# A two-layer hybrid decoder on one core: the first norm's scale and bias moved behind the transposition, throwaway products ahead, another order of first loads and splits

## The chip, the core and the metric

The kernel runs on one core of a Trainium2 chip. Its engines are TensorE (PE, with its weight loads as PEld), VectorE (DVE), ScalarE (ACT), GpSimd (POOL) and SyncE (SP, which here only issues DMAs). Each engine takes its instructions in the order in which the program issues them, and waits for the others by semaphores. The metric is the device time of one execution in microseconds; lower is better.

## The reference

Two layers of attention and gated MLP on 256 positions of 1,024 channels, with a LayerNorm ahead of the first layer and one behind each half of a layer:

```python
h = _layer_norm(x, ln_in_g, ln_in_b)              # the first norm
for l in range(DEPTH):                            # DEPTH = 2, ALPHA = 4 ** 0.25
    mix = _hybrid_mixer(h, positions, weights_of(l))   # x @ w_in, three attention branches, gates, w_out
    h = _layer_norm(ALPHA * h + mix, ln1_g[l], ln1_b[l])
    ffn = _conv_gated_mlp(h, w_up[l], conv_w[l], conv_b[l], w_down[l])
    h = _layer_norm(ALPHA * h + ffn, ln2_g[l], ln2_b[l])

def _layer_norm(x, g, b):                         # mean and var over the channels
    return (x - mean) * rsqrt(var + 1e-5) * g + b
```

The first norm's result is used twice: transposed, as the operand of all input projections of layer 0, and untransposed, in `ALPHA * h + mix`. Branch A of the mixer is softmax attention with a causal mask and a forget term: scores of a block of 128 queries, softmax, and the product with the values.

## The kernel before, in words

The 256 positions are two blocks (tb 0 and 1) of 128 rows; a block is held as two tiles of 128x512 (`h00`, `h01`, `h10`, `h11`). Products are made at nearly full fp32 precision from fp32r operands: each operand is split into a high half (ACT copies it with rounding) and a low half (DVE or POOL subtracts the high half from the original), and a product is three matmuls: high by high, low by high, high by low.

Weights are streamed from one flat array in order of use (class `Stream`): SP loads `raw` tiles (7 buffers), and each 128x512 piece is split into an `hl` tile (16 buffers; hl0 is the first piece). A `raw` buffer comes free when its pieces are split, an `hl` buffer when its products are done. `unit_x` takes 8 pieces and makes for both blocks a result of 128 rows by 512 columns: 48 matmuls of 128x512. `unit_x_tbfirst`, used for the first unit of each layer, makes all 24 of block 0 before those of block 1, since block 1's norm comes later.

The order of instructions is laid down when the program is built. `Tasks` holds generators for the side work (norms, rotary, softmax, ...); each `T.tick()` between matmuls advances every one by one step and lets the stream split another piece. `ready(...)` holds a task back by a rough clock of each engine (`Clocks`) until its inputs should be there. `T.until(cond)` ticks, without issuing products, until a condition holds. So what a task issues stands in the engine's queue wherever the building of the program was at the time, and the engine meets it there.

The start: ACT loads the identity, the positions and the rotary frequencies; SP loads block 0 of x, then `ln_in_g` and `ln_in_b` broadcast to all 128 rows, then two `raw` tiles, block 1, and more `raw`. `ln_half` makes the statistics, `ln_stats` the factor `rs` (a power on POOL), `ln_apply` four two-operand instructions of 128x512 on DVE with the broadcast scale and bias, and `ln_tail` transposes the tiles on PE (4 of 128x128 each, into a PSUM bank `att`), and writes the transposed operand as high half `hTh` (ACT) and low half `hTl` (DVE). Then `rotary_tables` (16 small POOL instructions and two sines on ACT between two table loads), the small loads and the mask constants follow.

Branch A (`task_A`) of layer 0 is added to the tasks behind the unit for its keys, and runs beside the unit for its values (`av`) and the first gate unit. Its scores, the transposition of the softmax's result `p` and the product with the values stand in PE's queue between the products of units. Behind `av` the program takes new `lng` and `lnb` tiles for the norm behind the mixer.

Of the kernel before, what the change touches and what calls it, by code (L numbers as in the profile page):

```python
# [10 lines left out]
F32 = mybir.dt.float32  # L11
R32 = mybir.dt.float32r
BF16 = mybir.dt.bfloat16
# [5 lines left out]
P = 128  # L19
# [89 lines left out]
class Stream:  # L109


    def __init__(self, nc, ve, sc, clocks, flat, raw_pool, hl_pool, plan):
        self.nc, self.flat, self.raw_pool, self.hl_pool = nc, flat, raw_pool, hl_pool
        self.ve, self.sc, self.clocks = ve, sc, clocks
        self.hold, self.low = False, LOW
        self.dma_clk, self.free_at, self.split_at = 0.0, {}, {}
        self.chunks, self.items = [], []
        off = 0
        for (_, _, kts, cols) in plan:
            n = kts * cols  # L120
            c = len(self.chunks)
            self.chunks.append((off, n))
            off += P * n
            w = 512 if cols >= 512 else cols
            for q in range(n // w):
                self.items.append((c, q * w, w))
        self.raw, self.hl = {}, {}
        self.next_dma = self.next_split = self.used = self.freed = 0

# [158 lines left out]
def tile_hybrid(ctx: ExitStack, tc: tile.TileContext, a: dict, out: bass.AP):  # L288
# [23 lines left out]
    def nm(s):  # L312
        uid[0] += 1
        return f"{s}_{uid[0]}"
# [25 lines left out]
    def bc_load(t, src, n, off=0, q=gp):  # L340
        q.dma_start(t, bass.AP(tensor=src.tensor, offset=off, ap=[[0, P], [1, n]]))
# [24 lines left out]
    for q in range(2):  # L366
        nc.sync.dma_start(h[0][q], xv[:, 0, 512 * q:512 * q + 512])
    for q in range(2):
        bc_load(lng[:, 512 * q:512 * q + 512], a["ln_in_g"], 512, 512 * q, nc.sync)
        bc_load(lnb[:, 512 * q:512 * q + 512], a["ln_in_b"], 512, 512 * q, nc.sync)  # L370
    W.dma()
    W.dma()
    for q in range(2):
        nc.sync.dma_start(h[1][q], xv[:, 1, 512 * q:512 * q + 512])
    nc.sync.dma_start(cst[:, C_TRI:C_INVF], a["cst"][:, C_TRI:C_INVF])
    for _ in range(RAW_BUFS - 2):
# [7 lines left out]
    def small_loads():  # L384
        bc_load(bf, a["b_f"], DEPTH * 4, q=nc.sync)
        bc_load(kvg, a["kv_norm_g"], DEPTH * LATENT, q=nc.sync)
        bc_load(dg, a["diff_norm_g"], DEPTH * P, q=nc.sync)
        nc.sync.dma_start(convp, a["convp"])

    tri = cst[:, C_TRI:C_TRI + P]  # L390
    negid = cpool.tile([P, P], BF16, name="negid")
    m01 = cpool.tile([P, 256], BF16, name="m01")
# [23 lines left out]
    def rotary_tables():  # L416

        c1 = 6.28125
        c2 = float(np.float32(np.float32((2 * math.pi - c1) * 2 ** 20).astype(np.int64) / 2.0 ** 20))
        c3 = float(np.float32(2 * math.pi - c1 - c2))  # L420
        gp.tensor_copy(posf, posi)
        for t in range(2):
            gp.tensor_scalar(ang[:, t, :], cst[:, C_INVF:C_INVF + 16], posf[:, t:t + 1], None, ALU.mult)
        gp.tensor_scalar(rn, ang, 1.0 / (2 * math.pi), 12582912.0, ALU.mult, ALU.add)
        gp.tensor_scalar(rn, rn, 12582912.0, None, ALU.subtract)
        for c in (c1, c2, c3):
            gp.tensor_scalar(red, rn, -c, None, ALU.mult)
# [5 lines left out]
        yield  # L433
# [93 lines left out]
    def ln_tail(tb, st, hT, g, b, flag):  # L527
# [11 lines left out]
        flag.add(tb)  # L539
        W.hold = len(flag) < 2  # L540


    def unit_x(lhs, kts, ncols):

# [10 lines left out]
    def unit_x_tbfirst(lhs, kts, ncols, ready=None):  # L555
        bk = [acc(), acc()]
        ws = []
        for tb in range(2):
            if ready is not None:
                T.until(lambda: tb in ready)  # L560
            for k in range(kts):
                if tb == 0:
                    ws.append(W.take())
                lh, ll = lhs(k, tb)
                mm3(bk[tb][:, :ncols], lh, ll, ws[k][:, 0, :ncols], ws[k][:, 1, :ncols], k == 0, k == kts - 1)
                if tb == 1:
                    W.free()
                T.tick()
        return bk

    def unit_w(hT, bks):
# [29 lines left out]
    def layer(l, hT, hflag):  # L601
# [585 lines left out]
        return hT2, flag2  # L1187


    hT, hflag = new_hT(), set()  # L1190
# [6 lines left out]
    T.tick()  # L1197
    tables = rotary_tables()
    next(tables)
    T.until(lambda: 0 in hflag)  # L1200
    for i in range(4):
        W.refill(ve)
    for q in range(2):
        ln_half(1, q, sts[1])
    T.add(ln_tail(1, sts[1], hT, lng, lnb, hflag))
    W.low = LOW
    for i in range(4):
        W.refill((gp, gp, ve, gp)[i])
        T.tick()
    T.add(tables)  # L1210
    small_loads()
    masks()

    def task_lambdas():
        for _ in range(40):
# [12 lines left out]
def lay_out(inp):  # L1228
# [3 lines left out]
    for l in range(DEPTH):  # L1232
# [13 lines left out]
        for (n, k0, kts, cols) in plan:  # L1246
            m = mats[n][k0 * P:(k0 + kts) * P, :].reshape(kts, P, cols)
            parts.append(m.transpose(1, 0, 2).reshape(-1))
    return np.concatenate(parts)


# [25 lines left out]
```

## Time and profile before

| | |
|---|---|
| three timed runs | 935.33 us median (933.94 to 935.53) |
| the profiled execution, its own time | 935.33 us |
| its span in the profile | 933.5 us |
| PE busy in the span | 905.1 us, 97% |
| DVE, ACT, POOL busy | 656.0, 513.5, 47.3 us |
| mean granted clock of TensorE | 0.995 |

A page of the profile gives each engine's busy time, and answers to queries give the instructions in order of time, who waited for whom, and what ended each wait. All times below are microseconds from the start of the span. Where one row stands for several instructions (x4), its time is that from the first's start to the last's end. PE's matmuls are pipelined, so a row's time is longer than the distance to the next; what a product costs is read from that distance.

### The profile page before, as it was taken

Reading aid. Unit: us, or ns where it says so; the run is one execution under the profiler, and the core shown is the slowest. Engines: PE = TensorE matmul, PEld = TensorE weight load, DVE = VectorE, ACT = ScalarE, POOL = GpSimd, SP = SyncE. Lnnn points to the kernel's source line nnn. Section 1 sums busy time; section 2 is a strip of 40 time slices with the busy share of each in tenths; the row PEclk is TensorE's granted clock in tenths of the full one; section 3 lists DMA queues with packets and bytes.
Section 4 is the critical chain, followed back from the end, with each engine's and each line's share of the span. In section 5 each row is a group of like instructions: output and inputs, shape, how many; then the busy total and the mean of one; then the engine's idle time right before and its main releaser. Section 6 shows DMA issues by size and latency. Waiting matters only on the chain.

```text
span 933.5 us, 14405 instructions
## 1 busy us (share of the span) xinstructions
PE 905.1 (97%) x5306; PEld 791.1 (85%) x5306; DVE 656.0 (70%) x1270; ACT 513.5 (55%) x1008; POOL 47.3 (5%) x62
## 2 busy tenths in 40 slices
PE   4999999999999999999999999999999999999995
PEld 2877897888888999999988789888888799999994
DVE  7788677567678766666788966865667886766755
ACT  4654666655536655655456455765554375655541
POOL 6000010001000000000010000100110100000001
PEclk9999999999999999999999999999999999999998
DMA  8843256656535766566345332846665286566601
GB/s 306 275 141 113 69 178 232 188 193 194 181 121 207 245 194 189 172 197 190 113 159 180 123 113 70 298 143 201 192 197 171 87 298 196 181 194 188 182 3 45
DMA packets 46536, 161.45 MB, mean 173 GB/s; under 512 B 5697, under 2 KB 6209, under 8 KB 46465
## 3 DMA queue, kind: packets, MB, share of 16 engines
q1 hardware_dynamic: 44208, 154.94, 51.5%
q0 software_dynamic: 1408, 4.98, 1.7%
q8 instruction: 41, 0.67, 0.3%
q10 hardware_dynamic: 848, 0.60, 0.2%
q14 instruction: 31, 0.25, 0.1%
HBM read 159.46 MB, written 1.05 MB: 172 GB/s over the span
## 4 chain that ended last, share of the span: by engine, by line
PE 70%; issue 21%; DVE 6%; DMA 1%; POOL 1%; ACT 0%; SPq 0%; ACTq 0%; DVEq 0%; POOLq 0%
PE acc L240 49%; PE att L240 21%; DVE h L240 2%; DVE s L240 1%; DMA raw<-in_w_dram 1%; POOL rs L240 1%; DVE hl L240 1%; DMA cst<-in_cst_dram 1%; DVE bst L240 1%; DVE mx L240 0%; DVE mv L240 0%; DVE hTl L240 0%; DVE t L240 0%; ACT h L240 0%; POOL hl L240 0%
## 5 line engine op out<-in xcount | busy, mean ns | idle before, releaser
L240 DVE TENSOR_TENSOR hl<-raw,hl 128x512 fp32r<-128x512 f32 (+1 forms) x581 | 389.5, 696 | 191.3 <-ACT hl L240 189.7
L240 ACT ACTIVATE hl<-raw 128x512 fp32r<-128x512 f32 (+1 forms) x584 | 347.8, 625 | 189.5 <-PE att L240 92.4
L240 PE MATMUL acc<-hl,hTh 128*128 128x512 f32 (+1 forms) x896 | 285.9, 392 | 4.1 <-DVE hl L240 2.0
L240 PE MATMUL att<-hTh,hl 128*128 128x256 f32 x1280 | 231.3, 283 | 0.0
L240 PEld LDWEIGHTS att<-hTh,hl 128*128 128x128 f32 x1280 | 200.8, 192 | 1.4
L240 PEld LDWEIGHTS acc<-hl,hTh 128*128 128x128 f32 x896 | 168.3, 189 | 39.5 <-DVE hl L240 2.7
L240 PE MATMUL att<-hTl,hl 128*128 128x256 f32 x640 | 181.1, 283 | 0.0
L240 PE MATMUL acc<-hl,hTl 128*128 128x512 f32 (+1 forms) x448 | 173.3, 387 | 1.8 <-DVE hTl L240 1.8
L240 PE MATMUL acc<-hl,act 128*128 128x512 f32 x528 | 123.4, 390 | 0.0
L240 PEld LDWEIGHTS att<-hTl,hl 128*128 128x128 f32 x640 | 122.8, 192 | 0.0
L240 PEld LDWEIGHTS acc<-hl,act 128*128 128x128 f32 x528 | 97.9, 188 | 19.5
L240 PEld LDWEIGHTS acc<-hl,hTl 128*128 128x128 f32 x448 | 85.0, 190 | 17.8 <-DVE hTl L240 2.7
L240 PE MATMUL acc<-hl,oT 128*128 128x512 f32 x288 | 68.0, 391 | 0.0
L240 PEld LDWEIGHTS acc<-hl,oT 128*128 128x128 f32 x288 | 53.8, 188 | 11.0
L240 DVE SCALAR_TENSOR_TENSOR cv<-att,convp,cv 128x255 f32<-128x255 f32 x88 | 40.4, 480 | 15.4 <-ACT cv L240 13.9
L240 PE MATMUL acc<-hTh,hl 128*128 128x256 f32 x256 | 47.7, 287 | 0.0
L240 PE MATMUL acc<-hl,mT 128*128 128x512 f32 x192 | 45.4, 392 | 0.0
L240 ACT ACTIVATE hTh<-att 128x512 fp32r<-128x512 f32 x16 | 9.6, 598 | 59.2 <-PE att L240 59.1
L240 PEld LDWEIGHTS acc<-hl,mT 128*128 128x128 f32 x192 | 35.6, 188 | 7.1
L240 PEld LDWEIGHTS acc<-hTh,hl 128*128 128x128 f32 x256 | 39.8, 191 | 2.0 <-issue 1.7
L240 PE MATMUL acc<-hTl,hl 128*128 128x256 f32 x128 | 36.2, 283 | 0.0
L240 POOL TENSOR_TENSOR rs<-mv,mhalf 128x1 f32<-128x1 f32 x10 | 9.1, 906 | 482.4 <-DVE mv L240 482.4
(160 smaller groups left out, 696.6 us busy)
## 6 DMA issues: line engine op xcount, KB each, us to landing
raw<-in_w_dram SPq DMA_DIRECT2D x284, 512.0 KB, 4.2
raw<-in_w_dram SPq DMA_DIRECT2D x8, 332.0 KB, 4.4
lng<-in_ln_g_dram POOLq DMA_DIRECT2D x4, 512.0 KB, 4.0
lnb<-in_ln_b_dram POOLq DMA_DIRECT2D x4, 512.0 KB, 5.9
h<-in_x_dram SPq DMA_DIRECT2D x4, 256.0 KB, 4.9
lng<-in_ln_in_g_dram SPq DMA_DIRECT2D x2, 256.0 KB, 5.2
lnb<-in_ln_in_b_dram SPq DMA_DIRECT2D x2, 256.0 KB, 5.2
wu<-in_w_ukv_dram POOLq DMA_DIRECT2D x2, 256.0 KB, 3.0
```

Source lines behind the costliest of these rows:

```text
L240: f(*args, **kw)
```

## The change

Six things change.

1. The first norm. `first_norm` takes the place of `ln_tail` for the norm ahead of layer 0. DVE makes only `(x - mean) * rs` (one `tensor_scalar` per tile of 128x512); PE transposes that; and on the transposed bank, where channels are rows, the scale and bias are one number per partition each (`gb`, 128x16, a small DMA on ACT's queue). They are applied in place in PSUM, 128 columns at a time: 4 `tensor_scalar` on DVE per bank, for the last bank 4 activations on ACT. High and low halves are made behind that.
2. `h` itself gets its scale and bias later: `first_residual`, a task that begins 180 ticks later, issues 8 `tensor_tensor` of 128x512 on DVE. Since `lng` and `lnb` are read there, `T.until(lambda: residual)` stands ahead of the place behind `av` where these tiles are taken anew.
3. Fifteen throwaway products (`spin`, bf16 ones, 128x128 by 128x512, into a bank that nobody reads) stand at the head of PE's queue.
4. The order of first loads: block 0, two `raw`, block 1, then `raw`; the broadcast `ln_in_g` and `ln_in_b` go behind the other small loads, ahead of the `raw` tiles that follow these on SP.
5. The order of the first splits: six of the first eight low halves go to POOL, ahead of the rotary tables, in place of three behind them; the masks are made 24 ticks later.
6. `unit_x_tbfirst` takes weights by fours, and issues the four high by high products, then the four low by high, then the four high by low (`mm3_group`). This holds for the first unit of both layers.

```diff
-    lng = hp.tile([P, D], F32, name="lng0", tag="lng")
-    lnb = hp.tile([P, D], F32, name="lnb0", tag="lnb")
+    gb = cpool.tile([P, 2, KD], F32, name="gb")
+    spin = cpool.tile([P, P], BF16, name="spin")
+    ve.memset(spin, 1.0)
     sc.dma_start(ident, a["cst"][:, C_ID:C_ID + P])
+    sc.dma_start(gb, bass.AP(tensor=a["w"].tensor, offset=W.total, ap=[[2 * KD, P], [KD, 2], [1, KD]]))
...
+    load_x(0, 3700)
+    W.dma_clk = 2300
     W.dma()
     W.dma()
+    load_x(1, 9000)
+    W.dma_clk += 1600
+    for _ in range(3):
+        W.dma()
     nc.sync.dma_start(cst[:, C_TRI:C_INVF], a["cst"][:, C_TRI:C_INVF])
...
         nc.sync.dma_start(convp, a["convp"])
+        bc_load(lng, a["ln_in_g"], D, q=nc.sync)
+        bc_load(lnb, a["ln_in_b"], D, q=nc.sync)
...
+    def first_norm(tb, st, hT, flag):
+        mu, rs = ln_stats(st)
+        if tb:
+            yield
+        for q in range(2):
+            ve.tensor_scalar(h[tb][q], h[tb][q], mu, rs, ALU.subtract, ALU.mult)
+        yield
+        bks = []
+        for q in range(2):
+            yield from ready("PE", h[tb][q])
+            bk = yield from att()
+            bks.append(bk)
+            transpose4(bk, h[tb][q])
+            for i in range(4):
+                o, k = bk[:, i * P:(i + 1) * P], 4 * q + i
+                if tb and q:
+                    sc.activation(o, o, AF.Identity, bias=gb[:, 1, k:k + 1], scale=gb[:, 0, k:k + 1])
+                else:
+                    ve.tensor_scalar(o, o, gb[:, 0, k:k + 1], gb[:, 1, k:k + 1], ALU.mult, ALU.add)
+        for q, bk in enumerate(bks):
+            split_out(hT[0][:, 4 * q:4 * q + 4, tb * P:(tb + 1) * P],
                      hT[1][:, 4 * q:4 * q + 4, tb * P:(tb + 1) * P],
                      bk.rearrange("p (k t) -> p k t", k=4))
+            att_free()
+            if not tb and not q:
+                W.split(gp)
...
+    def first_residual():
+        for _ in range(180):
+            yield
+        for tb in range(2):
+            for q in range(2):
+                y = h[tb][q]
+                while clocks.clk["DVE"] > clocks.clk["PE"]:
+                    yield
+                yield from ready("DVE", lng, lnb)
+                ve.tensor_tensor(y, y, lng[:, 512 * q:512 * q + 512], ALU.mult)
+                ve.tensor_tensor(y, y, lnb[:, 512 * q:512 * q + 512], ALU.add)
+                yield
+        residual.add(1)
+
+    def mm3_group(o, ls, ws, first, last):
+        n = len(ls)
+        for i, (lh, ll) in enumerate(ls):
+            mm(o, lh, ws[i][0], first and i == 0, False)
+        T.tick()
+        for i, (lh, ll) in enumerate(ls):
+            mm(o, ll, ws[i][0], False, False)
+        T.tick()
+        for i, (lh, ll) in enumerate(ls):
+            mm(o, lh, ws[i][1], False, last and i == n - 1)
+            if i % 2:
+                T.tick()
...
+        T.until(lambda: residual)
         lng = hp.tile([P, D], F32, name=nm("lng"), tag="lng")
...
+    warm = attp.tile([P, 512], F32, name=nm("att"), tag="att")
+    for _ in range(15):
+        mm(warm, spin, spin.unsqueeze(1).broadcast_to([P, 4, P]), True)
...
-    T.add(ln_tail(0, sts[0], hT, lng, lnb, hflag))
+    T.add(first_norm(0, sts[0], hT, hflag))
     T.tick()
+    for _ in range(3):
+        W.split(gp)
+    T.until(lambda: 0 in hflag)
+    for q in range(2):
+        ln_half(1, q, sts[1])
+    W.split(gp)
+    T.add(first_norm(1, sts[1], hT, hflag))
...
+    T.add(first_residual())
```

How the queues stand is seen from the built programs. A name is followed by numbers of its buffer; hl4 is the fifth weight piece, and of three rows on one `hl` with `hTh`, `hTl`, `hTh` the first is high by high, the second low by high, the third high by low.

POOL at the start of the program, before (the end of the rotary chain, and the first low halves):

```order
L240 TENSOR_SCALAR red_142<-ang_140 128x32
L240 TENSOR_SCALAR rn_141<-ang_140 128x32
L240 TENSOR_TENSOR red_142<-red_142,rn_141 128x32
L240 TENSOR_TENSOR hl4_209<-raw2_115,hl4_209 128x512
L240 TENSOR_TENSOR rs_10_215<-mv_9_212,mhalf_135 128x1
L240 TENSOR_TENSOR hl5_221<-raw2_115,hl5_221 128x512
L240 TENSOR_TENSOR hl7_229<-raw3_117,hl7_229 128x512
L240 DMA wu_11_241<-in_w_ukv_dram 128x512
```

and now (`rs_7` is block 0's factor, `rs_11` block 1's; the `CAST` begins the rotary chain):

```order
L241 TENSOR_TENSOR rs_7_172<-mv_6_169,mhalf_135 128x1
L241 TENSOR_TENSOR hl0_176<-raw0_106,hl0_176 128x512
L241 TENSOR_TENSOR hl1_179<-raw0_106,hl1_179 128x512
L241 TENSOR_TENSOR hl2_184<-raw1_108,hl2_184 128x512
L241 TENSOR_TENSOR hl3_207<-raw1_108,hl3_207 128x512
L241 TENSOR_TENSOR hl4_216<-raw2_112,hl4_216 128x512
L241 TENSOR_TENSOR rs_11_222<-mv_10_219,mhalf_135 128x1
L241 TENSOR_TENSOR hl6_231<-raw3_114,hl6_231 128x512
L241 CAST posf_139<-posi_95 128x2
```

The low halves moved ahead of the rotary chain, and five of them stand ahead of block 1's factor, in place of one.

PE in layer 0, branch A, before, at the transposition of the softmax's results (`p0`, `p1` are the two query blocks; the scores stand 31 rows higher, with products of hl73 to hl77 between):

```order
L240 MATMUL acc_176_1688<-hl77_1610,hTl_2_148 128x512
L240 MATMUL acc_176_1688<-hl77_1610,hTh_1_147 128x512
L240 MATMUL att_191_1791<-ident_98,p0_177_1700 128x128 x4
L240 MATMUL att_192_1796<-ident_98,p1_178_1701 128x128 x4
L240 MATMUL att_193_1801<-ident_98,p1_178_1701 128x128 x4
L240 MATMUL acc_175_1687<-hl78_1618,hTh_1_147 128x512
L240 MATMUL acc_175_1687<-hl78_1618,hTl_2_148 128x512
```

and now (the scores' last rows, the transposition, and the first two of the eight products with the values):

```order
L241 MATMUL att_179_1733<-m01_131,negid_130 128x2x128
L241 MATMUL att_179_1733<-augR_55_625,augL_54_624 128x512
L241 MATMUL att_179_1733<-t4_170_1601,t4_154_1377 128x256 x2
L241 MATMUL att_188_1768<-ident_96,p0_174_1718 128x128 x4
L241 MATMUL att_189_1773<-ident_96,p1_175_1719 128x128 x4
L241 MATMUL att_190_1778<-ident_96,p1_175_1719 128x128 x4
L241 MATMUL att_192_1787<-q0_186_1766,t4_173_1710 128x256
L241 MATMUL att_192_1787<-q1_187_1767,t4_173_1710 128x128
```

Between the scores and the transposition, and between that and the product with the values, no product of a unit stands any more; the six of hl72 that stood ahead of the scores come behind all of it too. DVE's queue has the 8 `tensor_tensor` of `first_residual` directly behind this stretch.

PE at the first unit of layer 1, block 0, where block 1's tiles `h10` and `h11` are transposed, before:

```order
L240 MATMUL acc_314_4795<-hl297_4680,hTh_303_4700 128x512
L240 MATMUL acc_314_4795<-hl297_4680,hTl_304_4701 128x512
L240 MATMUL acc_314_4795<-hl297_4680,hTh_303_4700 128x512
L240 MATMUL att_316_4820<-ident_98,h10_92 128x128 x4
L240 MATMUL acc_314_4795<-hl298_4694,hTh_303_4700 128x512
L240 MATMUL acc_314_4795<-hl298_4694,hTl_304_4701 128x512
L240 MATMUL acc_314_4795<-hl298_4694,hTh_303_4700 128x512
L240 MATMUL att_317_4833<-ident_98,h11_93 128x128 x4
L240 MATMUL acc_314_4795<-hl299_4812,hTh_303_4700 128x512
```

and now:

```order
L241 MATMUL acc_315_4833<-hl298_4732,hTh_304_4738 128x512
L241 MATMUL acc_315_4833<-hl299_4847,hTh_304_4738 128x512
L241 MATMUL att_317_4856<-ident_96,h10_92 128x128 x4
L241 MATMUL att_318_4863<-ident_96,h11_93 128x128 x4
L241 MATMUL acc_315_4833<-hl296_4707,hTl_305_4739 128x512
L241 MATMUL acc_315_4833<-hl297_4718,hTl_305_4739 128x512
L241 MATMUL acc_315_4833<-hl298_4732,hTl_305_4739 128x512
L241 MATMUL acc_315_4833<-hl299_4847,hTl_305_4739 128x512
L241 MATMUL acc_315_4833<-hl296_4707,hTh_304_4738 128x512
```

The transpositions stood behind 18 and 21 of block 0's 24 products, and stand behind 16 now, both together. Elsewhere in PE's queue, behind the first unit of layer 0, the rows are the same in both programs.

## Rows read from the trace of the kernel before

**Rows 1.** The page, part 1: busy time, share, instructions of PE.

```profile
PE 905.1 (97%) x5306; PEld 791.1 (85%) x5306; DVE 656.0 (70%) x1270; ACT 513.5 (55%) x1008; POOL 47.3 (5%) x62
```

**Rows 2.** PE's waits in the whole span: us in total, times, longest.

```profile
PE att L240 <- DVE h L240: 9.1, 3, 8.3
```

**Rows 3.** Busy time of a stretch: PE, PEld, DVE, ACT, POOL, granted clock, DMA share, GB/s.

```profile
17.60:24.00 6.40, 3.42 (x15) 2.10 (x13) 6.25 (x9) 3.54 (x6) 5.61 (x10) 0.87 0.81 257
```

**Rows 4.** Timeline, block 0's norm: start, us, engine, operation [idle before <- releaser].

```profile
5.80 0.55 POOL L240 TENSOR_TENSOR rs<-mv,mhalf 128x1 f32<-128x1 f32 x1 [5.37 <-DVE mv L240]
...
6.46 0.75 DVE L240 SCALAR_TENSOR_TENSOR h<-h,mv,lng 128x512 f32<-128x512 f32 x1 [0.74 <-DMA lng<-in_ln_in_g_dram]
...
8.34 1.11 PE L240 MATMUL att<-ident,h 128*128 128x128 f32 x4 [8.34 <-DVE h L240]
...
12.33 0.79 PE L240 MATMUL acc<-hl,hTh 128*128 128x512 f32 x1 [1.21 <-ACT hl L240]
```

**Rows 5.** Timeline, block 1's norm: its factor, POOL's low halves, and DVE beside them.

```profile
16.65 1.03 POOL L240 TENSOR_TENSOR rs<-mv,mhalf 128x1 f32<-128x1 f32 x1
...
17.65 2.94 POOL L240 TENSOR_TENSOR hl<-raw,hl 128x512 fp32r<-128x512 f32 x2
17.71 1.75 DVE L240 SCALAR_TENSOR_TENSOR h<-h,rs,lnb 128x512 f32<-128x512 f32 x1 [0.47 <-POOL rs L240]
```

**Rows 6.** Timeline of PE alone: products of the first unit, and the second's first.

```profile
24.90 1.03 PE L240 MATMUL acc<-hl,hTh 128*128 128x512 f32 x2
...
26.00 0.62 PE L240 MATMUL acc<-hl,hTh 128*128 128x512 f32 x2
26.47 0.40 PE L240 MATMUL acc<-hl,hTl 128*128 128x512 f32 x1
...
31.16 0.31 PE L240 MATMUL acc<-hl,hTl 128*128 128x332 f32 x1
```

**Rows 7.** DVE's groups by shape: count, busy us, mean ns, idle before.

```profile
L240 DVE TENSOR_TENSOR hTl<-att,hTh 128x512 fp32r<-128x512 f32 x16 | 10.7, 683 | 1.9 <-ACT hTh L240 1.9
...
L240 DVE TENSOR_SCALAR p<-p,rinv 128x256 f32<-128x256 f32 x16 | 4.9, 351 | 0.3
...
L240 DVE TENSOR_SCALAR p<-p,rinv 128x128 f32<-128x128 f32 x16 | 3.5, 283 | 0.1
```

**Rows 8.** ACT's groups by shape, in the same columns.

```profile
L240 ACT ACTIVATE hl<-raw 128x512 fp32r<-128x512 f32 x568 | 341.7, 629 | 189.5 <-PE att L240 92.4 <-DVE hl L240 50.9 <-PE acc L240 42.6
L240 ACT ACTIVATE cv<-att,convp 128x256 f32<-128x256 f32 x44 | 22.5, 561 | 7.5 <-PE att L240 5.9
...
L240 ACT ACTIVATE hTh<-att 128x512 fp32r<-128x512 f32 x16 | 9.6, 598 | 59.2 <-PE att L240 59.1
...
L240 ACT ACTIVATE oc<-att 128x128 f32<-128x128 f32 x16 | 4.2, 277 | 2.7 <-PE att L240 2.7
```

**Rows 9.** Timeline, branch A in layer 0, from its scores to its product.

```profile
152.79 0.69 DVE L240 TENSOR_REDUCE smx<-att 128x4 f32<-128x512 f32 x1 [1.26 <-PE att L240]
...
155.60 0.58 PE L240 MATMUL acc<-hl,hTh 128*128 128x512 f32 x1
...
156.06 1.28 DVE L240 TENSOR_REDUCE smx<-att 128x2 f32<-128x512 f32 x2
...
158.14 0.48 ACT L240 ACTIVATE p<-att,smx 128x256 f32<-128x256 f32 x1
...
162.62 1.47 PE L240 MATMUL att<-ident,p 128*128 128x128 f32 x12
...
165.32 2.78 PE L240 MATMUL att<-q,t 128*128 128x256 f32 x16
```

**Rows 10.** Timeline, the first unit of layer 1.

```profile
472.25 0.50 PE L240 MATMUL acc<-hl,hTl 128*128 128x512 f32 x1 [0.61 <-DVE hTl L240]
...
476.46 0.66 PE L240 MATMUL att<-ident,h 128*128 128x128 f32 x4
...
478.00 0.63 PE L240 MATMUL att<-ident,h 128*128 128x128 f32 x4 [0.19 <-DVE h L240]
```

More of the change, by code (lines that the diff above doesn't have):

```diff
@@ L126, in __init__ @@
                 self.items.append((c, q * w, w))
+        self.total = off
         self.raw, self.hl = {}, {}
@@ L359, in tile_hybrid, with load_x @@
     xv = a["x"].rearrange("o (t p) d -> p (o t) d", p=P)
-    lng = hp.tile([P, D], F32, name="lng0", tag="lng")
-    lnb = hp.tile([P, D], F32, name="lnb0", tag="lnb")
     ident = cpool.tile([P, P], F32, name="ident")
+    gb = cpool.tile([P, 2, KD], F32, name="gb")
+    spin = cpool.tile([P, P], BF16, name="spin")
+    ve.memset(spin, 1.0)
     sc.dma_start(ident, a["cst"][:, C_ID:C_ID + P])
+    sc.dma_start(gb, bass.AP(tensor=a["w"].tensor, offset=W.total, ap=[[2 * KD, P], [KD, 2], [1, KD]]))
     sc.dma_start(posi, a["positions"].rearrange("o (t p) -> p (o t)", p=P))
     sc.dma_start(cst[:, C_INVF:], a["cst"][:, C_INVF:])
[L366 to L370, printed above, removed]
+    def load_x(tb, at):
+        for q in range(2):
+            nc.sync.dma_start(h[tb][q], xv[:, tb, 512 * q:512 * q + 512])
+            clocks.done[h[tb][q].name] = at
+    load_x(0, 3700)
+    W.dma_clk = 2300
     W.dma()
     W.dma()
-    for q in range(2):
-        nc.sync.dma_start(h[1][q], xv[:, 1, 512 * q:512 * q + 512])
+    load_x(1, 9000)
+    W.dma_clk += 1600
+    for _ in range(3):
+        W.dma()
     nc.sync.dma_start(cst[:, C_TRI:C_INVF], a["cst"][:, C_TRI:C_INVF])
-    for _ in range(RAW_BUFS - 2):
+    for _ in range(RAW_BUFS - 5):
         W.dma()
@@ L388, in small_loads @@
         nc.sync.dma_start(convp, a["convp"])
+        bc_load(lng, a["ln_in_g"], D, q=nc.sync)
+        bc_load(lnb, a["ln_in_b"], D, q=nc.sync)
+    lng = hp.tile([P, D], F32, name="lng0", tag="lng")
+    lnb = hp.tile([P, D], F32, name="lnb0", tag="lnb")
     tri = cst[:, C_TRI:C_TRI + P]
@@ L432, in rotary_tables @@
         gp.tensor_tensor(red, red, rn, ALU.subtract)
-        yield
+        yield from ready("ACT", red)
         sc.activation(sn16[:, :, 16:32], ang, AF.Sin)
@@ L540, in ln_tail @@
         W.hold = len(flag) < 2
+    def first_norm(tb, st, hT, flag):
[19 more added lines that the diff above has]
+            split_out(hT[0][:, 4 * q:4 * q + 4, tb * P:(tb + 1) * P],
+                      hT[1][:, 4 * q:4 * q + 4, tb * P:(tb + 1) * P],
+                      bk.rearrange("p (k t) -> p k t", k=4))
+            att_free()
+            if not tb and not q:
+                W.split(gp)
+        flag.add(tb)
+        W.hold = len(flag) < 2
+    residual = set()
+    def first_residual():
[23 more added lines that the diff above has]
+                T.tick()
     def unit_x(lhs, kts, ncols):
@@ L560, in unit_x_tbfirst @@
                 T.until(lambda: tb in ready)
-            for k in range(kts):
+            for k in range(0, kts, 4):
                 if tb == 0:
-                    ws.append(W.take())
-                lh, ll = lhs(k, tb)
-                mm3(bk[tb][:, :ncols], lh, ll, ws[k][:, 0, :ncols], ws[k][:, 1, :ncols], k == 0, k == kts - 1)
+                    ws += [W.take() for _ in range(4)]
+                mm3_group(bk[tb][:, :ncols], [lhs(i, tb) for i in range(k, k + 4)],
+                          [(w[:, 0, :ncols], w[:, 1, :ncols]) for w in ws[k:k + 4]], k == 0, k + 4 == kts)
                 if tb == 1:
-                    W.free()
-                T.tick()
+                    W.free(4)
         return bk
@@ L1187, in layer @@
         return hT2, flag2
+    T.att += 1
+    warm = attp.tile([P, 512], F32, name=nm("att"), tag="att")
+    for _ in range(15):
+        mm(warm, spin, spin.unsqueeze(1).broadcast_to([P, 4, P]), True)
+    T.att -= 1
+    clocks.clk["PE"] = 6400.0
     hT, hflag = new_hT(), set()
@@ L1195, in tile_hybrid @@
     W.low = -1
-    T.add(ln_tail(0, sts[0], hT, lng, lnb, hflag))
+    T.add(first_norm(0, sts[0], hT, hflag))
     T.tick()
+    for _ in range(3):
+        W.split(gp)
+    T.until(lambda: 0 in hflag)
+    for q in range(2):
+        ln_half(1, q, sts[1])
+    W.split(gp)
+    T.add(first_norm(1, sts[1], hT, hflag))
+    T.tick()
+    W.split(ve)
+    T.tick()
+    W.split(gp)
+    W.split(ve)
+    W.low = LOW
     tables = rotary_tables()
     next(tables)
[L1200 to L1209, printed above, removed]
     T.add(tables)
     small_loads()
-    masks()
     def task_lambdas():
-        for _ in range(40):
+        for _ in range(24):
+            yield
+        masks()
+        for _ in range(16):
             yield
@@ L1248, in lay_out @@
             parts.append(m.transpose(1, 0, 2).reshape(-1))
+    parts.append(np.stack([inp["ln_in_g"].reshape(KD, P).T, inp["ln_in_b"].reshape(KD, P).T], axis=1).reshape(-1))
     return np.concatenate(parts)
```

## The prediction

> **What bounds the kernel now.** I read the page first: PE is busy 905.1 of 933.5 us [rows 1], so a change pays only where PE idles, and it costs wherever PE gets a new wait. Then PE's waits: most of the idle time is the wait for the normalized tiles at the start, 9.1 us of which 8.3 us is one wait [rows 2]. The timeline shows that start step by step: block 0's factor `rs` at 5.80, the first DVE instruction of the norm at 6.46 behind the load of `lng`, the transposition at 8.34, the first product at 12.33 [rows 4]; then block 1's norm, which shares DVE and POOL with the weight splits [rows 5]. The second unit (332 columns wide) begins at about 31.0, one product ahead of the row at 31.16 [rows 6]. From there PE is nearly always busy, so whatever brings that point forward is kept, unless a later wait takes it back. I therefore looked at the order of PE's queue in the changed program for new waits, and priced them from the rows at the same place: there are two, in branch A of layer 0 and at the first unit of layer 1.
>
> **The start, block 0.** `rs` comes as before at 5.80 + 0.55 = 6.35. The two `tensor_scalar` of 512 columns cost 0.49 us each: 283 ns at 128 columns and 351 at 256 make 68 ns per 128 more [rows 7]. The wait for `lng` and `lnb` goes; what is late next is `rs`. The tiles are ready at 6.95 and 7.45. The throwaway products need no input but a memset and start near 1.1. A pair of 512-column products takes 0.41 us longer at the lower clock (1.03 against 0.62), and at the full clock a product takes 0.47 / 2 = 0.23 us [rows 6], so at the lower clock 0.43. Fifteen take at most 6.5 us, to 7.6, and less once the clock rises: nothing or 0.6 us lost ahead of the transposition. At the full clock four transpositions take 0.65 us [rows 10] in place of 1.11 [rows 4], so the banks are full at 7.7 and 8.4. Then 8 `tensor_scalar` on PSUM. No row shows that form; from below it is 0.28 us [rows 7], from above the 0.56 us of a scale and bias on ACT with 256 columns [rows 8]. I take 0.33, near the first: 2.6 us, to 10.4. `hTh` takes 0.60 [rows 8] and `hTl` 0.68 [rows 7]; the first products start at 9.8 in place of 12.33 and low by high can run at 11.2.
>
> **The start, block 1.** Here the new order costs. Splitting is no longer in front of PE on DVE, but POOL has five low halves ahead of block 1's factor, at 2.94 / 2 = 1.47 us beside DVE's work [rows 5]; I take 1.35, since DVE reads PSUM for most of this time. They start at 7.5, when hl0's high half (0.63 us [rows 8]) is there, and end at 14.2; the factor, at 1.03 us [rows 5], is there at 15.2. POOL's next instruction is hl6's low half, with its inputs ready. Exactly this stands in the trace: DVE's instruction behind `rs` took 1.75 us beside POOL's low half, where 0.75 is its usual time [rows 4, 5]. So `h10` is done at 17.1 and `h11` at 17.6. PE has the products of hl0 to hl7 with block 0's high half done by 13.9 and waits behind the transposition, 3 us. Both banks are full at 18.4; the four activations with scale and bias lie between 0.28 (128 columns without) and 0.56 (256 columns with) [rows 8], taken as 0.43, 1.7 in all, and the first `hTh` stands behind them on ACT: block 1's products start at 20.9. The 24 at 0.23 us end at 26.4. Against 31.0 that is **4.6 us gained**. By the bounds: 6.9 if DVE isn't held (1.3 us), the four activations take 0.28 (0.6) and the scalings on PSUM 0.28 (0.4); 3.0 if the clock is low for 3 us of block 1's products (1.6).
>
> The Trainium skill, page "SBUF — State Buffer", section "Who interferes with whom", says that a `tensor_scalar` in a two-port mode and a GpSimd instruction exclude each other for a whole instruction, and whoever issues first goes on. The row shows such a hold, but for a two-operand instruction. By that rule the hold of 1.3 us stays in the sum; without it the start would gain 5.9 us.
>
> The rest of the start is hidden. The sines on ACT now wait for a rotary chain that begins behind hl6 on POOL (about 16.7), and ACT's splits of the second unit stand behind them; they are back at about 26, as the second unit needs hl9, so 0 to 0.6 us. The 1 MB of broadcast `lng` and `lnb` on SP stands ahead of the `raw` that unit three needs some 15 us later.
>
> **Branch A of layer 0.** In the trace the products of hl73 to hl77 cover the softmax. They are gone from there. PE resumes behind the scores at 155.60, with nothing of its own that isn't the softmax's [rows 9]. DVE reduces the first block at 152.79 and the second from 156.06 to 157.34, ACT's last exponential ends at 158.14 + 0.48 = 158.62; I allow 0.3 us for the two short instructions behind it (the sum's read and a reciprocal, each nearer to an instruction of few columns than to the 0.28 of 128), and two scalings of 256 columns (0.35 each [rows 7]) end at 159.6. These hang on the scores alone, so they keep their distance. Then 8 transpositions at 1.47 / 12 = 0.12 us end at 160.6, the copies out of PSUM (0.60 on ACT, 0.68 on DVE) at 161.2, and the product with the values, 2.78 less the 0.23 that overlaps with the next product, at 163.75. Without waits the 12 transpositions and that product end at 155.60 + 1.2 + 2.55 = 159.35. So **4.4 us lost**, 3.6 to 4.6 by how the copies fall. Nothing gives it back: PE was fully busy there. The 8 `tensor_tensor` behind it (8 x 0.68 = 5.5 us on DVE by the nearest row [rows 7]) cost nothing, since 16 split pieces, hl72 to hl87, lie ahead of PE, 16 x 6 x 0.23 = 22 us; without that store they would cost 5.5.
>
> **The clock.** Between 17.60 and 24.00 PE was busy 3.42 of 6.40 us, and the granted clock fell there to the lower level, 1.2 GHz (mean 0.87) [rows 3]; the products up to about 25.7 ran at it [rows 6]. Branch A's new stretch from 155.60 to 161.2 holds 1.4 us of work in 5.6, less than that. I expect the clock to fall once: some 3 us of the following work at double time, **1.4 us lost**, 0 if it holds, 1.7 at most.
>
> **The first unit of layer 1.** The grouping hides the wait of 0.61 us for `hTl` [rows 10] behind three more products, but the transpositions of block 1 now stand ahead of 8 of block 0's products and not of 3. They wait for DVE's `h11` at 478.00 as before, and 5 more products come behind: 5 x 0.23 = **1.15 us lost**, since the time that they left free ahead of 478.00 is idle. If the clock falls there too, 1.6 more.
>
> **The sum.** 4.6 gained, 4.4 + 1.4 + 1.15 lost: 2.35 us slower. The profiled execution took 935.33, which is also the median, so about 937.7.
>
> **The rivals.** (1) No change that can be measured: the start gains 5.9 because the one-input `tensor_scalar` isn't held by POOL, or the clock holds in branch A; 5.9 - 4.4 - 1.4 - 1.15 is 1.05 slower, the clock alone gives 0.95 slower, and both 0.35 faster: 935.0 to 936.4. For it: no row shows a one-input instruction held. Against it: the new stretch is as empty as the one in which the clock fell. (2) Faster, by block 1's chain alone: factor, tiles and scale run without any hold, so that block 1's products start at 18.6 in place of 20.9 and the unit ends at 24.1, and branch A costs 3.6 with the clock up: 6.9 - 3.6 - 1.15 = 2.15 faster, 933.2. It decides where block 1's products start ahead of 18.9. For it speaks that PE's 9.1 us wait is the largest in the trace; against it POOL's five low halves. (3) The throwaway products don't lift the clock, or it falls again ahead of block 1, and also at layer 1: 3.0 gained, 4.6 + 1.7 + 2.75 lost, 6 slower, 941.3. The clock's fall at 17.60 to 24.00 speaks for it, the short gaps in layer 1 against.
>
> **How the numbers follow.** The forecast has 0.42, rival 1 0.28, rival 2 0.20, rival 3 0.10. Within 0.2%, 1.9 us either way, this kernel can't be told from no change. The forecast's own spread is 936.3 to 939.5, so a fourth of it falls inside; slower is 0.32 + 0.10 and 0.02 of rival 1, 0.44; faster is rival 2 less what of it stays inside, and a little of what no row shows, 0.20; the rest, 0.36, is no change. The range leaves out a tenth on each side: 932.6 to 940.4.
>
> **What would show it.** In the changed profile: the first product near 9.8 and at 0.23 us spacing; DVE's `tensor_scalar` on `h10` as long as POOL's low half beside it; the second unit at 26.4; in branch A a PE idle of about 3 us between the transposition of `p0` and that of `p1`, named as a wait for DVE, and a clock at half behind it; waits of 1.5 and 1.1 us for `h` at the first unit of layer 1. The prediction is wrong if PE runs through branch A, or if the second unit starts ahead of 24.5.

## The result and the profile after

The changed kernel takes 941.86 us (median of 4 runs, 941.08 to 942.86); the kernel before takes 935.43 us beside it (4 runs, 933.94 to 935.57). The ratio is 1.0071, interval 1.0059 to 1.0083: 6.4 us slower, where 2.35 were forecast. The profiled executions took 941.08 and 935.33 us, so 5.75 us are to be found in the two traces.

Page, part 1, of the changed kernel, which answers to [rows 1]:

```profile
span 939.3 us, 14454 instructions
...
PE 912.3 (97%) x5321; PEld 794.2 (85%) x5321; DVE 659.9 (70%) x1284; ACT 516.3 (55%) x1012; POOL 49.3 (5%) x65
```

PE's waits in the whole span (total, times, longest), which answer to [rows 2]:

```profile
PE att L241 <- DVE h L241: 3.4, 5, 1.2
PE att L241 <- ACT hl L241: 2.9, 1, 2.9
PE acc L241 <- ACT hTh L241: 2.8, 2, 2.2
PE att L241 <- DVE t L241: 2.6, 3, 1.4
PE att L241 <- DVE p L241: 2.3, 2, 2.0
```

The 9.1 us for `h` have become 3.4. In their place stand 2.9 us put down to one of ACT's split pieces, 2.8 for `hTh` and 2.3 for the softmax's `p`, which the kernel before did not have. To see where each costs, take three PE instructions that both programs share and that wait for the same thing in both. The kernel before:

```profile
74.41 0.85 PE L240 MATMUL att<-ident,t 128*128 128x128 f32 x6 [1.41 <-DVE t L240]
281.89 0.50 PE L240 MATMUL acc<-hl,hTl 128*128 128x512 f32 x1 [0.60 <-DVE hTl L240]
529.70 0.74 PE L240 MATMUL att<-ident,t 128*128 128x128 f32 x5 [1.25 <-DVE t L240]
```

The changed kernel:

```profile
72.53 0.74 PE L241 MATMUL att<-ident,t 128*128 128x128 f32 x5 [1.42 <-DVE t L241]
285.18 0.50 PE L241 MATMUL acc<-hl,hTl 128*128 128x512 f32 x1 [0.58 <-DVE hTl L241]
535.35 0.52 PE L241 MATMUL att<-ident,t 128*128 128x128 f32 x3 [0.86 <-DVE t L241]
```

(The counts of the transpositions differ only because the rows are cut off at other places; each is a row of eight.) The differences are 1.88 us ahead, then 3.29 behind, then 5.65 behind. So the start gave 1.88, the stretch with branch A lost 5.17, and the stretch with layer 1's first unit lost 2.36 (after a wait that is 0.39 shorter). The forecast had 4.6, 5.8 and 1.15.

**The start** follows the forecast to the second unit and not behind it. The timeline of the changed kernel:

```profile
1.04 6.29 PE L241 MATMUL att<-spin 128*128 128x512 bf16 x15 [1.04 <-DVE spin L241]
...
7.17 1.04 PE L241 MATMUL att<-ident,h 128*128 128x128 f32 x8
...
7.81 3.46 DVE L241 TENSOR_SCALAR att<-att,gb 128x128 f32<-128x128 f32 x8 [0.60 <-PE att L241]
...
10.38 2.07 PE L241 MATMUL acc<-hl,hTh 128*128 128x512 f32 x4 [2.17 <-ACT hTh L241]
...
15.32 1.95 DVE L241 TENSOR_SCALAR h<-h,mv,rs 128x512 f32<-128x512 f32 x2 [0.45 <-POOL rs L241]
...
20.47 1.20 PE L241 MATMUL acc<-hl,hTh 128*128 128x512 f32 x4 [0.58 <-ACT hTh L241]
...
21.29 1.28 ACT L241 ACT_TABLE_LOAD   x1
...
22.59 0.23 ACT L241 ACTIVATE sn<-ang 128x32 f32<-128x32 f32 x1
...
23.05 1.28 ACT L241 ACT_TABLE_LOAD   x1
...
24.34 4.79 ACT L241 ACTIVATE hl<-raw 128x332 fp32r<-128x332 f32 x11
...
26.19 0.31 PE L241 MATMUL acc<-hl,hTl 128*128 128x332 f32 x1
...
29.04 1.05 ACT L241 ACTIVATE t<-acc 128x512 f32<-128x512 f32 x2
...
31.25 0.42 DVE L241 TENSOR_TENSOR ru<-t,cc 128x256 f32<-128x256 f32 x1
...
32.68 1.06 PE L241 MATMUL att<-ident,t 128*128 128x128 f32 x8 [2.88 <-ACT hl L241]
```

The row of 332 columns at 26.19 is the one that stood at 31.16 [rows 6]: 5.0 us ahead. But the first unit's result, complete at about 26.2, is copied by ACT only at 29.04. ACT is an in-order queue. It left for the sines at 21.29 (two table loads of 1.28 us) and came back at 24.34, and then eleven split pieces stand ahead of the copy. The rotation on DVE begins at 31.25, and PE stands 2.88 us before the transposition of `t`. (The row names ACT's split piece, which ends at about the same time; in e5 below, where the same wait is 2.84 us, it names DVE's `t`.) In the kernel before, that transposition came without a wait:

```profile
34.62 1.03 PE L240 MATMUL att<-ident,t 128*128 128x128 f32 x8
```

So of the 5.0 us at the second unit 1.9 are left here.

**Branch A**, PE's timeline of the changed kernel, which answers to [rows 9]:

```profile
152.56 0.74 PE L241 MATMUL att<-ident,p 128*128 128x128 f32 x4
155.30 0.50 PE L241 MATMUL att<-ident,p 128*128 128x128 f32 x2 [2.00 <-DVE p L241]
156.12 1.03 PE L241 MATMUL att<-ident,p 128*128 128x128 f32 x6 [0.33 <-DVE p L241]
157.59 4.28 PE L241 MATMUL att<-q,t 128*128 128x256 f32 x16 [0.44 <-DVE q L241]
```

No product of a unit stands between the scores and the product with the values: 2.77 us of idle PE, and then a product that takes 4.28 us in place of 2.78. **Layer 1's first unit**, which answers to [rows 10]:

```profile
479.75 0.66 PE L241 MATMUL att<-ident,h 128*128 128x128 f32 x4 [1.19 <-DVE h L241]
481.29 1.04 PE L241 MATMUL att<-ident,h 128*128 128x128 f32 x4 [0.89 <-DVE h L241]
481.99 2.05 PE L241 MATMUL acc<-hl,hTl 128*128 128x512 f32 x4
```

Behind both places the clock is at its lower level, 1.2 GHz (the sixth value after the stretch's length is the granted clock):

```profile
157.10:160.50 3.40, 2.96 (x10) 2.58 (x10) 0.34 (x1) 0.60 (x1) 0.00 (x0) 0.50 0.00 0
...
481.40:484.80 3.40, 3.40 (x11) 2.81 (x12) 2.75 (x6) 2.43 (x7) 0.00 (x0) 0.50 0.55 154
```

### The profile page after: what moved, and what is told of

Same layout as the page of the kernel before. It is cut to its first block, busy times and chain, and to the rows that moved or that the text cites. A ratio compares the mean times of both kernels' runs of the same rounds, so it can differ in the third digit from the quotient of the medians.

```text
span 939.3 us, 14454 instructions
## 1 busy us (share of the span) xinstructions
PE 912.3 (97%) x5321; PEld 794.2 (85%) x5321; DVE 659.9 (70%) x1284; ACT 516.3 (55%) x1012; POOL 49.3 (5%) x65
## 3 DMA queue, kind: packets, MB, share of 16 engines
HBM read 159.47 MB, written 1.05 MB: 171 GB/s over the span
## 4 chain that ended last, share of the span: by engine, by line
PE 67%; issue 22%; DVE 7%; ACT 3%; POOL 1%; DMA 1%; DVEq 0%; POOLq 0%; ACTq 0%
PE acc L241 46%; PE att L241 21%; DVE h L241 2%; DVE s L241 1%; ACT hl L241 1%; POOL rs L241 1%; DVE hl L241 1%; DMA raw<-in_w_dram 1%; ACT t L241 0%; DVE bst L241 0%; DVE t L241 0%; ACT p L241 0%; DVE att L241 0%; ACT L241 0%; DVE mx L241 0%
## 5 line engine op out<-in xcount | busy, mean ns | idle before, releaser
L241 PE MATMUL acc<-hl,hTh 128*128 128x512 f32 (+1 forms) x896 | 279.4, 390 | 2.8 <-ACT hTh L241 2.8
L241 PE MATMUL acc<-hl,hTl 128*128 128x512 f32 (+1 forms) x448 | 170.3, 389 | 1.2 <-DVE hTl L241 1.2
```

Source lines behind the costliest of these rows:

```text
L241: f(*args, **kw)
```

## Experiments

Ten kernels ran, each timed beside the kernel before, whose median was 935.3 to 935.5 each time. The first four change one thing of the changed kernel.

**e1: the residual's scale and bias earlier.**

```diff
-        for _ in range(180):
+        for _ in range(100):
```

> The changed kernel, with the scale and bias of h given to VectorE after 100 of the program's ticks in place of 180, so that they are done before branch A and the wait for them ahead of the second layer-norm tables finds nothing to wait for; branch A gets its products of the weights back between scores and transpositions. Theory (branch A is the largest loss): the changed kernel's trace has 2.8 us of idle TensorE there and 3.41 us at the lower clock, 5.2 us in all, so 941.9 - 5.2 = 936.7 us. Rival (VectorE's eight instructions, 5.5 us, cost wherever they stand, since VectorE is nearly as late in the new place): 939 us or more, with a new TensorE wait for hl or t between 60 and 100 us.

Measured: 936.24 us, ratio to before 1.0015 (1.0006 to 1.0023), 5.6 less than the changed kernel. The theory holds. PE has its products of the weights behind the scores again (row 156.33 of its timeline: `acc<-hl,hTh`, no idle time), and no new wait stands between 60 and 100 us. From the row of `t` at 75.13 to the row of `hTl` at 282.62 its trace has 207.49 us, as the kernel before (207.48). So branch A's loss is the place where the program waits for the residual, not the residual's work.

**e2: the old order in layer 1.** `unit_x_tbfirst` gets a flag `group`; without it the loop is the old one with `mm3` for each weight.

```diff
-        bk = unit_x_tbfirst(lhs, KD, 512, hflag)
+        bk = unit_x_tbfirst(lhs, KD, 512, hflag, l == 0)
```

> The changed kernel, with the products of layer 1's first unit in the old order (three products per weight tile); layer 0's first unit keeps the groups of four weights. Theory (the groups cost in layer 1): the two waits for h, 1.19 and 0.89 us, go back to 0.61 for hTl and 0.19 for h, and the clock doesn't fall at 481 us, 1.3 + 1.5 us; 0.4 us of it is lost at the later wait for t at 535 us, which grows back to 1.25: 941.9 - 2.4 = 939.5 us. Rival (the fall of the clock at 481 us comes from the work before, not from the two waits): 940.9 us.

Measured: 940.41 us, 1.0059 (1.0047 to 1.0072), 1.45 less. The direction is right and the size lies between theory and rival. e1 shows why: there the groups were still in, the two waits were there, and the clock did not fall behind them (PE's timeline):

```profile
477.19 0.66 PE L241 MATMUL att<-ident,h 128*128 128x128 f32 x4 [1.19 <-DVE h L241]
478.73 0.63 PE L241 MATMUL att<-ident,h 128*128 128x128 f32 x4 [0.89 <-DVE h L241]
479.12 1.17 PE L241 MATMUL acc<-hl,hTl 128*128 128x512 f32 x4
```

The same waits, then four products in 1.17 us and not 2.05. From the row of `hTl` to that of `t` (285.18 to 535.35 in the changed kernel, 250.17 us) e1 takes 248.56 and e2 247.44. So the groups cost about 1.1 us by their waits, and some 1.6 more in those executions in which the clock falls. The theory's smaller term did not come: in e2 the wait for `t` at the end of that stretch is 0.89 us and did not grow back to 1.25, so it is shorter than before for another reason than layer 1's groups, which the runs don't show.

**e3: the sines' table first.**

```diff
+    sc.preload_act_table_set("trig_and_small")
...
         yield from ready("ACT", red)
+        for _ in range(3):
+            yield
         sc.activation(sn16[:, :, 16:32], ang, AF.Sin)
         sc.activation(cc16[:, :, 0:16], red, AF.Sin, bias=half_pi)
-        sc.preload_act_table_set("natural_log_exp_and_others")
...
     def task_lambdas():
-        for _ in range(24):
+        for _ in range(20):
+            yield
+        sc.preload_act_table_set("natural_log_exp_and_others")
+        for _ in range(4):
             yield
```

The first line stands at ACT's head; the second table's load moves 20 ticks into a later task.

> The changed kernel; ScalarE loads the table of the sines at its head in place of the first load, the two sines stand three splits later, and the table of the exponential is loaded behind hl20, when the second unit's splits are done. Theory (the 2.9 us wait at 32.7 us is ScalarE's detour for the sines, 21.29 to 24.34, which makes the splits of the second unit and the copy of the first unit's result late): most of it goes, 2.0 to 2.9 us, to 939.0 to 939.9 us, and the first product of the second unit stays at 26.1. Rival (the splits are late because ScalarE and VectorE need 0.44 and 0.49 us for each of 332 columns and TensorE takes 0.45 us): the wait stays over 2 us and the time at 941.5.

Measured: 940.81 us, 1.0066 (1.0052 to 1.0080), 1.05 less. On ACT's detour the theory is right, since the wait shrinks from 2.88 to 0.34 us, but little of it arrives. PE's timeline of e3:

```profile
30.53 1.06 PE L241 MATMUL att<-ident,t 128*128 128x128 f32 x8 [0.34 <-ACT hl L241]
42.54 0.82 PE L241 MATMUL att<-ident,t 128*128 128x128 f32 x6
44.65 0.39 PE L241 MATMUL att<-cst,lf 128*16 128x128 f32 x2 [1.29 <-DVE lf L241]
```

A new wait of 1.29 us stands at 44.65. ACT's own waits from 20 to 60 us say what is behind it:

```profile
ACT hl L241 <- DMA raw<-in_w_dram: 1.7, 1, 1.7
```

ACT now waits for a landing: the next weights (`raw11`) stand on SP's queue behind the small loads and the 1 MB of `lng` and `lnb`. e3 alone does not show that these loads are the cause; e7 does.

**e4: without the throwaway products** (the loop of 15 `mm` left out).

> The changed kernel without the fifteen throwaway products. Theory (they give no more than the first transpositions at the full clock, since the clock falls again at 10.31 us while TensorE waits for ScalarE): the eight transpositions take 2.2 us in place of 1.04, of which 0.6 to 1.1 us reaches the end: 942.5 to 943.0 us, with the first four or five us of products at the lower level as now. Rival (they cost by nothing and bring nothing): 941.9 us. Second rival (the clock's fall at 10.31 follows from the throwaway products, as work followed by idling; without them the products of block 0 run at the full clock sooner): 941 us or less.

Measured: 941.61 us, 1.0069 (1.0057 to 1.0082). No difference in time. In its trace the eight transpositions take 1.97 us and the second unit begins 0.7 us later (at 26.88), but in this execution the clock did not fall in branch A, so that a loss of this size can hide. The second rival did not come: the first four products of block 0 take 2.08 us (at 11.10), no less than with the throwaway products. It is taken up again in e9.

The next four put edits together: e5 two of these, and each of the others one more.

**e5: e1 and e2 together**, so that the start alone is left.

> The changed kernel with both the residual's instructions after 100 ticks and the old order in layer 1's first unit, so that what is left of the change is the start. Theory (the two losses are apart and add up, and the start's 4.9 us up to the second unit shrinks to 1.9 us at the wait for t at 32.7 us): 941.9 - 5.6 - 1.5 = 934.8 us, 0.5 faster than the kernel before; between 933.4 and 935.0. Rival (the start gives nothing or loses): 935.4 or more.

Measured: 934.44 us, 0.9990 (0.9981 to 0.9999). The two losses very nearly add up: layer 1's old order gives 1.8 us behind e1 and 1.45 alone (e2), and the time lies 0.4 below the 934.8 that the sum of e1 and e2 gave. The start gives 1.0 us in the medians, 2.1 in the profiled executions, with the 2.84 us wait for `t` still in it.

**e6: e5 with e3.**

> As e5_start_alone, with the sines' table first on ScalarE and the sines three splits later (e3). Theory (behind the sines the next limit is the landing of the weights: ScalarE waited 5.9 us for raw in e3, whose gain of 2.5 us at the wait for t shrank to 0.5 us at 44.65 and 52.2 us): 1 us less than e5, 933.8. Rival (e3's gain was small by its clock falling elsewhere, and the 2.5 us are kept): 932.3.

Measured: 932.98 us, 0.9977 (0.9967 to 0.9987), 1.5 less than e5. As the theory says, and 0.5 more; between 20 and 60 us ACT waits 2.0 us for `raw` (1.7 in e3; the 5.9 of the expectation have the waits at the program's head in them), and PE 1.55 for `lf`.

**e7: the broadcast loads later.**

```diff
     def small_loads():
...
-        bc_load(lng, a["ln_in_g"], D, q=nc.sync)
-        bc_load(lnb, a["ln_in_b"], D, q=nc.sync)
...
     def first_residual():
-        for _ in range(100):
+        for _ in range(50):
+            yield
+        bc_load(lng, a["ln_in_g"], D, q=nc.sync)
+        bc_load(lnb, a["ln_in_b"], D, q=nc.sync)
+        for _ in range(50):
             yield
```

> As e6_start_and_sines, with the broadcast loads of the first norm's scale and bias (512 KB each) taken from SP's queue ahead of raw11 and issued after 50 ticks, behind raw23, where the DMA queues move only 105 GB/s. Theory (the 1 MB in front of the weights makes ScalarE's splits from hl22 on late; 1 MB at the 410 GB/s of this stretch is 2.6 us): the waits at 44.65 and 52.2 us shrink and 1.5 to 2.5 us is gained against e6: about 932. Rival (the chain of short instructions from the second unit's result to lf and t is what TensorE waits for there, whatever the weights do): the same as e6 within 0.3 us.

Measured: 931.37 us, 0.9959 (0.9947 to 0.9972), 1.6 less than e6. The theory holds: between 20 and 60 us ACT no longer waits for `raw`, and PE has no wait at `lf`; the one behind it, 0.79 us in e6, is 0.49 (timeline of e7):

```profile
42.84 0.39 PE L241 MATMUL att<-cst,lf 128*16 128x128 f32 x2
...
49.93 0.41 PE L241 MATMUL att<-ident,t 128*128 128x128 f32 x2 [0.49 <-DVE t L241]
```

In the changed kernel SP issues the two loads at 20.20 and 20.68 us, and behind them the DMA is full; in e7 it issues them at 51.20 and 51.67, where the changed kernel's DMA is about a quarter as busy (stretches of the changed kernel; the last two values are the DMA's share and GB/s):

```profile
24.00:28.00 4.00, 4.00 (x24) 3.64 (x23) 3.14 (x8) 3.99 (x11) 0.47 (x4) 1.00 1.02 342
...
50.00:55.00 5.00, 4.63 (x23) 3.54 (x22) 3.95 (x16) 3.29 (x8) 0.54 (x1) 1.00 0.27 53
```

**e8: hl6's low half on VectorE.**

```diff
     W.split(ve)
     T.tick()
-    W.split(gp)
+    W.split(ve)
     W.split(ve)
```

> As e7_broadcasts_later, with the low half of hl6 on VectorE behind the two tensor_scalar of block 1 and not on GpSimd beside them. Theory (GpSimd's low half holds VectorE's tensor_scalar: the pair took 1.95 us beside it and 1.00 without): h10 is ready 1 us sooner, the pair takes 1.0 us, and the rotary chain starts 1.3 us sooner on GpSimd; VectorE has 0.69 us more ahead of the scalings of block 1, so block 1's products start 0.3 to 0.9 us sooner, and 0.3 us or less reaches the end. Rival (the tensor_scalar takes 0.95 us for each for another reason, as VectorE's own reads): the pair stays near 1.9 us and the time the same or 0.5 slower.

Measured: 930.67 us, 0.9950 (0.9938 to 0.9963); its interval overlaps e7's. What the theory says of the pair is right. DVE's timeline of e7, then of e8:

```profile
15.24 1.94 DVE L241 TENSOR_SCALAR h<-h,mv,rs 128x512 f32<-128x512 f32 x2 [0.45 <-POOL rs L241]
```

```profile
15.99 1.00 DVE L241 TENSOR_SCALAR h<-h,mv,rs 128x512 f32<-128x512 f32 x2 [0.46 <-POOL rs L241]
```

In e7 POOL's low half ran from 15.17 to 16.44 beside the pair. The 0.94 us did not reach the end of the start, since in e8's execution the factor came 0.75 us later: ACT's first split waited for its weights until 8.04 us and not 7.04, so that POOL's five low halves, 6.2 us long in both, ended at 14.99 and not at 13.96. This need not be the edit's doing: in e10, with the same low half on DVE, the first split starts at 6.74. The second unit's row stands at 26.32 in e8 and at 26.15 in e7. Whether the 0.7 us between the medians are real is open.

**e9: e8 without the throwaway products.**

> As e8_low_half_on_vector, without the fifteen throwaway products; there the later waits, at which e4's difference could hide, are gone. Theory (they give the first transpositions the full clock, 1.97 us in e4 against 1.04, and the second unit began 0.8 us later in e4): 0.5 to 0.9 us slower than e8, 931.2 to 931.6. Rival (block 1's chain on VectorE and GpSimd sets the second unit and TensorE waits for it either way): 930.7, no difference.

Measured: 930.74 us, 0.9953 (0.9939 to 0.9966): the rival. PE's timeline, the slow transpositions and the second unit:

```profile
7.21 1.11 PE L241 MATMUL att<-ident,h 128*128 128x128 f32 x4 [7.21 <-DVE h L241]
8.62 1.12 PE L241 MATMUL att<-ident,h 128*128 128x128 f32 x4 [0.30 <-DVE h L241]
...
20.57 1.19 PE L241 MATMUL acc<-hl,hTh 128*128 128x512 f32 x4 [0.76 <-ACT hTh L241]
...
26.30 0.31 PE L241 MATMUL acc<-hl,hTl 128*128 128x332 f32 x1
```

The products of block 1 start at 20.57 in e8 too. The time that the throwaway products give block 0 goes into the wait for block 1.

**e10: e8 with the old order in layer 0 too.** The flag of e2 is False for both layers.

> As e8_low_half_on_vector, with the old order of the products (three per weight tile) in layer 0's first unit too, so that nothing of the groups of four is left. Theory (TensorE has the products' high parts to do while hTl and the low halves are made, and this is what the groups buy): the first low product waits for hTl from 10.5 to 11.9 us and later ones for GpSimd's low halves, 1 us later at the second unit: 931.2 to 931.7. Rival (block 1's chain bounds the second unit, and TensorE waited 0.6 + 0.96 us for it): 930.7 or less, with the waits ahead of block 1 smaller by what is lost in block 0.

Measured: 930.76 us, 0.9952 (0.9939 to 0.9964): the rival again. The first low product waits 1.14 us for `hTl`, as the theory says, but the second unit's row stands at 25.90, 0.4 us ahead of e8. Nothing of the groups pays, in either layer.

e8, e9 and e10 are the fastest of this study, 0.5% faster than the kernel before. e9 and e10 leave out one part of the change each and lose nothing by it; a kernel without both was not tried.

## Why the prediction was wrong

**The step that failed is "The rest of the start is hidden."** It gave 0 to 0.6 us for the sines, since ACT would be back at about 26, "as the second unit needs hl9". ACT was back at 24.34, sooner than that. But I asked only who needs the next piece on ACT, and not what else is queued behind the sines: the copy of the first unit's result, eleven pieces later, and behind it the rotation and PE's transposition of `t`. That cost 2.88 us. The traces say the start gave 1.88 us and not 4.6; 2.7 of the 3.4 us between forecast and profiled time are this step. Of the others, layer 1 adds 1.2, branch A takes back 0.6, and 0.1 comes behind 535 us. In the medians the miss is 4.1; the 0.7 beyond the traces isn't placed.

The 1 MB of `lng` and `lnb` was costed at nothing in the same paragraph. In the changed kernel ACT waited only 0.4 us for it, as the detour in front was longer; no run moves the two loads alone. e3 and e7 show its own price once the detour is gone: 1.6 us. From e5 to e7 the whole step is priced, 3.1 us, and with it out of the way the start gives 4.1 us in the medians (935.45 to 931.37), near the 4.6 forecast.

**Block 0 and block 1** came as forecast, by errors that cancel. The scalings on PSUM took 0.43 us each and not 0.33 (8 in 3.46 us), so the first product came at 10.38 and not 9.8. Block 1's products started at 20.47 (20.9 forecast), and the second unit's row lies 5.0 us ahead (4.6 forecast). The hold of `tensor_scalar` by POOL, which the forecast took from a two-operand row, is real: 1.95 us for block 1's pair in the changed kernel, and in the experiments 1.94 for it beside a low half and 1.00 without one (e7, e8).

The Trainium skill, page "SBUF — State Buffer", section "Who interferes with whom", states such an exclusion for a `tensor_scalar` in a two-port mode, which the earlier trace showed for a two-operand instruction alone. e7 and e8 agree with it by 0.94 us; that this `tensor_scalar` runs in such a mode, no run shows. The page says too that whoever issues first goes on. That fits, as POOL's piece began at 15.17 and DVE's pair at 15.24.

**Branch A**: 5.8 forecast, 5.17 measured. e4's execution kept its clock there (granted 1.00 from 157.0 to 160.5, 0.51 in the changed kernel), and its two rows separate the terms:

```profile
74.42 0.85 PE L241 MATMUL att<-ident,t 128*128 128x128 f32 x6 [1.41 <-DVE t L241]
...
285.64 0.50 PE L241 MATMUL acc<-hl,hTl 128*128 128x512 f32 x1 [0.60 <-DVE hTl L241]
```

From the one to the other are 211.22 us, 207.48 in the kernel before and 212.65 in the changed one: 3.74 by the waits (4.4 forecast, 3.6 to 4.6) and 1.43 by the clock (1.4 forecast). Only 2.8 of the 3.74 stand as idle time in PE's rows; where the rest lies they don't say. The mechanism holds, and both sizes within their ranges.

**Layer 1**: the waits of 1.19 and 0.89 us were forecast as 1.5 and 1.1. Without the fall they cost about 1.1 (e1 against e2; 1.15 forecast). The fall of the clock, which the forecast left at "1.6 more" outside the sum, did come in the profiled execution and cost 1.6. The wait for `t` at 535 us, 0.4 shorter, takes the two together down to 2.36: 1.2 us of the miss.

**The rivals.** Rival 3 had the right size, 941.3, and one of its terms, the clock in layer 1; but it let the start shrink through the clock. The clock did fall in block 0 (four products in 2.07 us at 10.38), and that cost nothing, since PE waits for block 1 behind it: e9 is slower there than e8, and e10 has its products of block 0 at 0.23 us, and all three take the same time. Rival 2 and one arm of rival 1 needed a DVE that is not held, and fell with the pair's 1.95 us. The other arm of rival 1, a clock that holds in branch A, came in e4's execution, which took 939.99 us all the same.

What stays open: in the medians the start alone gives 1.0 us (e5) and in the profiled executions 2.1. e5's runs spread from 933.1 to 935.7, and the clock goes with it: its mean over a run is 0.995 in the four runs of 933.1 to 933.3 us and 0.990 to 0.992 in the four of 935.1 to 935.7. Where it falls in these isn't known, since only one execution of each kernel has a trace; in e1's it is at 0.76 from 17 to 24 us, in block 1's products, and the transposition of `t` comes at 75.13 there, where e5, whose program is the same up to there, has it at 72.58. Which of the parts 1, 4 and 5 of the change gives the start its gain was not tried apart.

## What to carry to other kernels

When PE is brought forward at one place, follow every in-order queue from there, not for its next instruction but for the last one that PE will ask of it: a detour of 3 us on ACT is paid by the copy eleven instructions behind it. When a wait for data off the path is written as a point of the program's order (here `T.until` for the residual), ask what can no longer be issued in its place; doing that work 80 ticks sooner gave back 5.6 us. And the next limit can stand right behind the first: the sines were worth 1.5 us, and behind them the landing of weights 1.6.

## What the runs showed of the hardware

- The same wait does not always bring the clock down. In branch A the granted clock fell in the changed kernel, e2 and e3 and not in e4; in layer 1 behind waits of 1.2 and 0.9 us it fell in the changed kernel and e3 and not in e1 and e4; in block 0 behind a wait of 2.1 to 2.4 us it fell in the changed kernel and e8 and not in e3 and e10. One fall cost 1.43 us in branch A; in layer 1 the stretch from the row at 285.18 to that at 535.35 is 1.6 us longer than the same stretch of e1.
- The fifteen throwaway products took 0.42 us each (6.29 us) to the last one, against 0.23 for a 512-column product at the full clock [rows 6], though PE was busy without a gap; the transpositions behind them ran at the full clock. Taken alone their rows are 0.63 us long, and a bf16 row of the same size at 147.62 us is 0.39. Yet the granted clock stands at 1.00 in that stretch, and also where e9's first transpositions take 1.11 us in place of 0.65 [rows 10]. So at the program's head the column doesn't seem to show the lower level.
- `tensor_scalar` on PSUM with 128x128 takes 0.43 us on DVE, against 0.28 in SBUF [rows 7]; four activations with scale and bias there take 1.83 us on ACT, 0.46 each.
